# A fused attention-and-MLP layer on Trainium2: a pair's last values are transposed within the next projection, and the high parts of the projections' weights are made in two pieces

## The chip, the cores and the metric

The kernel runs on one core of one Trainium2 chip. The metric is the device time of one execution in microseconds. Before the change three timed runs gave a median of 1065.94 us (1065.62 to 1066.48).

## The reference: what is computed

One layer on a sequence of 1024 tokens of width 1024, all in float32:

```
n  = rms_norm(h, norm1_g)
qa, ka, va, qb, kb, vb = split(n @ w_in)     # 512, 128, 128, 512, 512, 512 columns
ya = mixer_a(qa, ka, va, sinks)              # 8 heads, 2 key heads, window 128, ALiBi, sinks
yb = mixer_b(qb, kb, vb, rel_bias)           # 8 heads, own chunk of 64 and 8 before, learned bias
h  = h + concat(rms_norm(ya), rms_norm(yb)) @ w_out
h  = h + square(relu(rms_norm(h) @ w_ff1)) @ w_ff2
out = rms_norm(h)
```

Both mixers are softmax attention with heads of 64 columns. In group B each query block of 128 rows looks at up to five key blocks.

## The kernel before

**Numbers in two parts.** Every operand of a matmul is kept as a high part (rounded to the format that TensorE reads, `fp32r` in the profile) and a low part (what is left). One product is three matmuls into one accumulator: high by high, high by low, low by high (`mm3`, L129 in the profile). High parts are made by ScalarE (ACT), low parts by VectorE (DVE) or GpSimd (POOL) in `split_l` (L135).

**Stages.** Up to about 46 us the input is loaded and the first projections are made; up to about 394 us attention runs, interleaved with projections; then the second half of the output projection, the first MLP matmul up to about 752 us and the second up to the end.

**Projections.** `in_proj` makes one of queries, keys or values for a pair of heads. It loads a weight of 128x8x128, has ACT make its high part in one instruction of 128x1024 (L172, `w_qB<-st_qB`), POOL its low part in four of 128x256 (L135, through `load_weight`), and then goes over two halves of the tokens and eight k blocks: three matmuls into an accumulator `ip_` per block. Each block is one step of the generator. At the end of a half, `place` scales the result by the tokens' norm on DVE (`ts_`, L246 for values). Values must be turned to have tokens on the partitions: `turn_v` transposes four blocks on TensorE (`vt_`, L132), ACT copies the high part out (L269, `VvB`), DVE subtracts for the low part (L135, `VvB`). The first half's values are turned within the second half at k block 2. The second half's are turned after two empty steps, and so right ahead of the next projection's first matmuls. Fifteen projections go through `in_proj`: the queries of A's pairs 1 to 3, and keys, queries, values (kB, qB, vB) of B's four pairs.

**Attention.** `UnitA` and `UnitB` are pieces of attention. For each block of queries there are scores (`S_`), a bias and a row minimum on DVE (`P_`, L412 or L414), the exponential on ACT (L415), the division by the row sum on DVE or POOL (L589, L521), transposes of the probabilities on TensorE (`pt_`), their eviction in two parts, ACT first and DVE second (`T_`, L422 and L135), and the products with the values (`av_`). A `pt_` of group B, numbered 0 to 7 within a unit, is filled by up to four transposes, and is free again only when ACT and DVE have both read it.

**What sets the order.** TensorE's order is the program's order, held by hand (`pe_order`). A queue `Filler` deals out steps of projections between the steps of attention: `interleave` runs one step of a unit, sometimes a score of the next, and then some filler steps. `finish(name)` runs filler until a pair's projections are done. The last projection in the queue is followed by `out_proj_a`, the first half of the output projection (`op_A_`). The order on ACT, DVE, POOL and on SP's queue of DMAs is chosen by the Tile scheduler. In group B's stage accumulators `ip_` or `op_A_`, `pt_` and `vt_` share three PSUM banks (tag `w`, `bufs=3`), handed out by rotation as the scheduler finds them free.

**Places.** The second half of a B pair's values is turned four times: at about 145 us (pair 0, within group A's last units; called place 1), 202 us (pair 1, place 2), 260 us (pair 2, place 3) and 316 us (pair 3, place 4, where the filler has come to `op_A_`).

Of the kernel before, what the change touches and what calls it, by code (L numbers as in the profile page):

```python
# [45 lines left out]
def kernel(  # L46
# [26 lines left out]
    nc = tc.nc  # L73
# [10 lines left out]
    def page(shape, name, dt=F32R):  # L84
        return main.tile(shape, dt, tag="pg", bufs=NPAGES, name=name)
# [69 lines left out]
    def mm3(ps, a, b, start, stop, shared=False):  # L155

        matmul(ps, a[0], b[0], start=start, stop=False, skip_group_check=shared)
        matmul(ps, a[0], b[1], start=False, stop=False, skip_group_check=shared)
        matmul(ps, a[1], b[0], start=False, stop=stop, skip_group_check=shared)

    def load_weight(src, shape, name, low_engine, cuts=1, pieces=1):

        st = stage(shape, f"st_{name}")
        w = [page(shape, f"w{hl}_{name}") for hl in range(2)]

        def steps():
            n = shape[1] // cuts
            for i in range(0, shape[1], n):
                load(st[:, i : i + n], src[:, i : i + n])
                for j in range(i, i + n, n // pieces):  # L170
                    c = slice(j, j + n // pieces)
                    nc.scalar.activation(w[0][:, c], st[:, c], AF.Copy)  # L172
                    width = shape[2] if len(shape) > 2 else 1
                    short = min(n // pieces, LOW_COLS // width) if low_engine is nc.gpsimd else n // pieces
                    for k in range(j, j + n // pieces, short):
                        c = slice(k, k + short)
                        split_l(low_engine, w[1][:, c], st[:, c], w[0][:, c])
                yield

        if cuts > 1:  # L180
            return w, steps()
        for _ in steps():
            pass
        return w
# [47 lines left out]
    def project(acc, w, t, ks=range(NK)):  # L232
        for k in ks:
            n = [nT[t][hl][k // 2][:, k % 2, :] for hl in range(2)]
            mm3(acc, (w[0][:, k], w[1][:, k]), n, k == 0, k == NK - 1)

    def place(acc, kind, name, dst, t, low_engine, st=None):
        if st is not None:
            pass
        elif name == "vA":  # L240
            st = page([P, 2, HALF], f"ts_{name}_{t}")
        else:
            st = main.tile([P, 2, HALF], F32R, tag="tst", bufs=2, name=f"ts_{name}_{t}")
        c = slice(t * HALF, (t + 1) * HALF)
        if kind == "v":
            nc.vector.tensor_tensor(f(st[:, 0]), acc, R1[:, c], ALU.mult)  # L246
            return lambda *where: turn_v(st, name, dst, t, *where)
        if kind[0] == "q":
            nc.vector.scalar_tensor_tensor(f(st[:, 1]), acc, HD**-0.5, R1[:, c], ALU.mult, ALU.mult)
        else:  # L250
            nc.vector.tensor_tensor(f(st[:, 1]), acc, R1[:, c], ALU.mult)
        nc.scalar.activation(st[:, 0], f(st[:, 1]), AF.Copy)
        split_l(low_engine, st[:, 1], f(st[:, 1]), st[:, 0])
        for hl in range(2):
            for s in range(2):
                src = f(st[s * HD : (s + 1) * HD, hl])
                if kind == "q":
                    last = nc.sync.dma_start(f(dst[s][hl * HD : (hl + 1) * HD, c]), src)
                else:
                    for rep in range(2):  # L260
                        last = nc.sync.dma_start(f(dst[2 * hl + s][rep * HD : (rep + 1) * HD, c]), src)
        return last.ins.name
# [9 lines left out]
    def proj_weight(c0, name, low_engine, *cuts):  # L272
        return load_weight(w_in[:, c0 : c0 + P].rearrange("(k p) c -> p k c", p=P), [P, NK, P], name, low_engine, *cuts)
# [10 lines left out]

    def in_proj(c0, kind, name, dst, new):

        w = proj_weight(c0, name, nc.gpsimd)
        yield
        later = None
        for t in range(2):  # L290
            acc = aps.tile([P, HALF], F32, tag="w", bufs=3, name=f"ip_{name}_{t}")
            for k in range(NK):
                project(acc, w, t, (k,))
                if k == 2 and later:
                    later(aps, "w", 3)
                if k == NK - 1:
                    if t == 0:
                        dst.extend(new(name))
                    later = place(acc, kind, name, dst, t, nc.gpsimd)
                    later = later if kind == "v" else None  # L300
                yield
        if later:
            yield
            yield
            later(aps, "w", 3)

    dve, pool = nc.vector, nc.gpsimd
    KA, VA, Q = new_k("A"), new_v("A"), new_q("A0")
# [42 lines left out]
    project(accs[1], wts[1], 1)  # L351
    Qs = [Q, [], [], []]
    ahead_A1 = in_proj(QA0 + P, "q", "qA1", Qs[1], new_q)
    next(ahead_A1)
    last_load[0] = turns[1]
# [10 lines left out]
    aps = ap_.enter_context(tc.tile_pool(name="aps", bufs=1, space=PSUM, reuse_waits="tile"))  # L366
# [60 lines left out]
    class Pair:  # L427
# [34 lines left out]
        def finish(self, t):  # L462

            Y, yc = self.out[t]
            c = slice(t * HALF, (t + 1) * HALF)
            if self.j == 0 and t == 0:
                sq[self.kind] = page([P, SEQ], f"sq{self.kind}", F32)
            acc = sq[self.kind][:, c]
            if self.j == 0:
                nc.gpsimd.tensor_tensor(acc, Y, Y, ALU.mult)  # L470
            elif self.m == 7 and t == 1:
                nc.scalar.activation(yc, Y, AF.Square)
                nc.vector.tensor_tensor(acc, acc, yc, ALU.add)
            else:
                y2 = page([P, HALF], f"y2{t}_{self.m}", F32)
                nc.gpsimd.tensor_tensor(y2, Y, Y, ALU.mult)
                nc.gpsimd.tensor_tensor(acc, acc, y2, ALU.add)
            if self.y is None:
                y = page([P, 2, HALF], f"y{t}_{self.m}")
                split_y(y, Y, self.m)  # L480
                nc.sync.dma_start(yd[self.m, :, t], f(y))
            else:
                split_y(self.y[t], Y, self.m)
# [176 lines left out]
    def load_y(m):  # L660
        y = new_y(m)
        for t in range(2):
            nc.sync.dma_start(f(y[t]), yd[m, :, t])
        return y

    def out_weight(m):
        return load_weight(w_out[m * P : (m + 1) * P, :], [P, D], f"o{m}", pool, 1, 2)
# [3 lines left out]
    def out_proj_step(ps, ys, ws, q, tb, c):  # L671
        y = ys[q][tb // 4][:, :, tb % 4 * P : (tb % 4 + 1) * P]
        mm3(ps, (y[:, 0], y[:, 1]), [v[:, c] for v in ws[q]], q == 0, q == 3)

    class Filler:
# [28 lines left out]
                self.step()  # L704

        def finish(self, name):
            while any(q[0] == name for q in self.queue):
                self.step()

    def interleave(unit, nexts, n_fill):  # L710
# [11 lines left out]
    def out_proj_a():  # L722
        ys, ws = [], []
        for m in range(4):
            ws.append(out_weight(m))
            if m > 1:
                ys += [load_y(2 * m - 4), load_y(2 * m - 3)]
        yield
        for tb in range(TB):
            h = hres[tb] = page([P, D], f"h{tb}", F32)  # L730
            nc.sync.dma_start(h, x[tb * P : (tb + 1) * P, :])
            for dh in range(2):
                c = slice(dh * HALF, (dh + 1) * HALF)
                ps = aps.tile([P, HALF], F32, tag="w", bufs=3, name=f"op_A_{tb}_{dh}")
                for q in range(4):
                    out_proj_step(ps, ys, ws, q, tb, c)
                    if q == 3:
                        nc.vector.scalar_tensor_tensor(h[:, c], ps, rA[:, tb : tb + 1], h[:, c], ALU.mult, ALU.add)  # L738
                    yield
# [4 lines left out]
    for j in range(4):  # L744
        if j > 1:
            fill.add(f"A{j}", in_proj(QA0 + j * P, "q", f"qA{j}", Qs[j], new_q))
        pair = Pair("A", j, Qs[j], KA, VA)
        units += [(UnitA(pair, i0), f"A{j}", A_FILL) for i0 in range(0, TB, 2)]
    y7 = new_y(7)
    for j in range(4):  # L750
# [4 lines left out]
        pair = Pair("B", j, Q, K, V, y7 if j == 3 else None)  # L755
        units += [(UnitB(pair, s, t), f"B{j}", B_FILL[t] if j < 3 else LAST_FILL[t][s]) for t in range(2) for s in range(2)]
    fill.add("out", out_proj_a())

    ahead = []
# [460 lines left out]
    g, p, n0 = order2[-GQ]  # L1220
# [57 lines left out]
```

## Time and profile before

| | before |
|---|---|
| median of three runs | 1065.94 us |
| the profiled execution, its own time | 1066.38 us |
| its span in the trace | 1064.5 us |
| TensorE (PE) busy | 1047.2 us, 98% |
| DVE busy | 707.2 us, 66% |
| ACT busy | 578.7 us, 54% |
| POOL busy | 415.9 us, 39% |
| mean granted clock of TensorE | 0.999 |

The time of the execution is 1.9 us over the span; what lies around the span is taken as constant. In a timeline's row stand the start in us, the busy time in us, the engine, the line, the operation and its tile as output<-input; `x4` means that four alike in a row are put together; brackets give the idle time of the engine ahead of it and what ended that. The table of waits adds such idle time by what was waited for.

### The profile page before, as it was taken

What the parts mean: (1) busy time and instruction counts of PE and PEld (TensorE: products, weight loads), DVE (VectorE), ACT (ScalarE), POOL (GpSimd) and SP (SyncE); (2) the same over time, 40 slices, a digit from 0 to 9 for tenths busy, and PEclk for the clock granted to TensorE, in tenths of its full rate; (3) what the DMA queues carried; (4) which work ended last, traced back from release to release, by engine and by line L of the source; (5) the groups of instructions that cost most, each with busy time, mean ns of one, the idle gap of its engine ahead of it and who ended that gap; (6) DMA issues with size and microseconds to landing.
All of it is one profiled execution on the core that took longest, in us unless ns stands there. A gap on an engine that the chain in (4) does not pass through costs nothing.

```text
span 1064.5 us, 14392 instructions
## 1 busy us (share of the span) xinstructions
PE 1047.2 (98%) x5040; PEld 873.0 (82%) x5040; DVE 707.2 (66%) x1134; ACT 578.7 (54%) x994; POOL 415.9 (39%) x316
## 2 busy tenths in 40 slices
PE   8999999999999999999999999999999999999997
PEld 6888877888888888888888888888888888888885
DVE  4577887767677765696524335436878777778667
ACT  7676765666574566675544544455533333333346
POOL 1476765244370243405564454345014024024025
PEclk9999999999999999999999999999999999999999
DMA  9955525253575442214544535417997535532004
GB/s 327 265 145 138 160 79 156 92 141 102 136 249 207 139 159 100 96 63 164 192 139 159 177 119 172 164 63 247 376 403 269 164 123 164 181 116 89 1 1 159
DMA packets 90440, 170.17 MB, mean 160 GB/s; under 512 B 7808, under 2 KB 43520, under 8 KB 90368
## 3 DMA queue, kind: packets, MB, share of 16 engines
q1 hardware_dynamic: 90224, 169.25, 48.4%
q8 instruction: 40, 0.66, 0.3%
q14 instruction: 32, 0.26, 0.1%
q10 hardware_dynamic: 144, 0.00, 0.0%
HBM read 105.26 MB, written 45.09 MB: 141 GB/s over the span
## 4 chain that ended last, share of the span: by engine, by line
PE 89%; DVE 5%; DMA 2%; ACT 1%; issue 1%; SPq 0%; POOL 0%; DVEq 0%; ACTq 0%
PE f L129 27%; PE f_a L129 16%; PE f_c L129 8%; PE op_B L129 4%; PE f_b L129 4%; PE op_A L129 4%; PE ip_qB L129 4%; PE ip_qA L129 4%; PE ip_vB L129 3%; PE av_B L129 3%; PE ip_kB L129 3%; PE pt_B L132 2%; PE S_B L129 2%; PE S_A L129 1%; DMA xs<-in_xT_dram 1%
## 5 line engine op out<-in xcount | busy, mean ns | idle before, releaser
L129 PE MATMUL f<-X,W 128*128 128x512 f32 x1344 | 306.0, 389 | 0.0
L129 PEld LDWEIGHTS f<-X,W 128*128 128x128 f32 x1344 | 252.0, 188 | 52.8 <-DVE X L135 0.5
L129 PE MATMUL f_a<-V,U 128*128 128x512 f32 x768 | 176.0, 389 | 0.0
L129 PEld LDWEIGHTS f_a<-V,U 128*128 128x128 f32 x768 | 144.2, 188 | 29.9
L135 POOL TENSOR_TENSOR U<-u,U 128x1024 fp32r<-128x1024 f32 x32 | 79.8, 2494 | 227.4 <-PE f_c L129 135.9
L135 POOL TENSOR_TENSOR W<-T,W 128x1024 fp32r<-128x1024 f32 x29 | 74.7, 2577 | 138.9 <-ACT W L946 138.9
L129 PE MATMUL f_c<-V,U 128*128 128x512 f32 x384 | 88.3, 389 | 0.0
L129 PEld LDWEIGHTS f_c<-V,U 128*128 128x128 f32 x384 | 72.1, 188 | 15.0
L946 ACT ACTIVATE V<-Z 128x1024 fp32r<-128x1024 f32 x32 | 33.9, 1060 | 88.9 <-PE f_a L129 44.6
L135 POOL TENSOR_TENSOR W<-w,W 128x1024 fp32r<-128x1024 f32 x23 | 58.2, 2532 | 32.5 <-ACT W L946 32.0
L135 DVE TENSOR_TENSOR V<-w,V 128x1024 fp32r<-128x1024 f32 x24 | 50.3, 2096 | 30.1 <-ACT V L946 30.1
L946 ACT ACTIVATE V<-w 128x1024 fp32r<-128x1024 f32 x24 | 25.4, 1060 | 80.8 <-issue 34.2
L995 DVE TENSOR_TENSOR k<-f,k 128x1024 f32<-128x1024 f32 x24 | 29.3, 1221 | 59.6 <-PE f L129 59.6
L946 ACT ACTIVATE U<-u 128x1024 fp32r<-128x1024 f32 x56 | 58.5, 1044 | 10.4 <-DMA ud<-k 7.1
L415 ACT ACTIVATE P_B<-P_B,nm_B 128x640 f32<-128x640 f32 (+2 forms) x64 | 44.4, 694 | 25.2 <-DVE nm_B L414 13.1
L989 ACT ACTIVATE k<-f 128x1024 f32<-128x1024 f32 x24 | 24.6, 1026 | 59.2 <-PE f L129 59.2
L135 DVE TENSOR_TENSOR V<-Z,V 128x1024 fp32r<-128x1024 f32 x32 | 48.4, 1516 | 9.3 <-ACT V L946 5.9
L129 PE MATMUL op_A<-w_o,y 128*128 128x512 f32 x192 | 52.1, 397 | 0.5 <-DVE h L738 0.5
L129 PE MATMUL ip_vB<-nT,w_vB 128*128 128x512 f32 x192 | 51.9, 398 | 0.0
L946 ACT ACTIVATE W<-T 128x1024 fp32r<-128x1024 f32 x32 | 33.9, 1059 | 32.9 <-PE f L129 20.7
L129 PE MATMUL ip_qB<-nT,w_qB 128*128 128x512 f32 x192 | 51.5, 396 | 0.0
L129 PE MATMUL ip_kB<-nT,w_kB 128*128 128x512 f32 x192 | 51.3, 396 | 0.0
(212 smaller groups left out, 2031.7 us busy)
## 6 DMA issues: line engine op xcount, KB each, us to landing
w<-in_w_ff_dram SPq DMA_DIRECT2D x64, 512.0 KB, 4.5
u<-ud SPq DMA_DIRECT2D x56, 512.0 KB, 4.4
ud<-k SPq DMA_DIRECT2D x48, 512.0 KB, 3.1
KkB<-ts_kB SPq DMA_DIRECT2D x64, 128.0 KB, 2.3
yd<-y SPq DMA_DIRECT2D x14, 512.0 KB, 2.8
y<-yd SPq DMA_DIRECT2D x14, 512.0 KB, 6.5
xs<-in_xT_dram SPq DMA_DIRECT2D x16, 256.0 KB, 5.5
xr<-in_x_dram SPq DMA_DIRECT2D x8, 512.0 KB, 7.1
```

The costliest lines, as they stand in the source:

```text
L129: pe(nc.tensor.matmul(*args, **kw))
L132: pe(nc.tensor.transpose(*args))
L135: engine.tensor_tensor(lo, full, f(hi), ALU.subtract)
L415: nc.scalar.activation(pr[:, :n], pr[:, :n], AF.Exp, bias=nm, scale=-1.0, accum_out=sm)
L946: nc.scalar.activation(w[0], full, AF.Copy)
L989: nc.scalar.activation(kept[p], ps, AF.Copy)
L995: dve.tensor_tensor(v, ps, v, ALU.add)
```

## The change: when the last values are turned, and the weight's high part in two

First, `in_proj` no longer turns the second half's values itself. It appends the turning to a list `pending`, and `turn_pending` runs it at k block 2 of the next projection, or at the third product of `out_proj_a`. `finish(name)` also steps until the pair's entry is gone from the list. Two empty steps after a values projection stay. Second, `proj_weight` is called with `cuts=1, pieces=2`: ACT makes the high part in two instructions of 128x512, and POOL's first two low parts depend on the first of them alone. There are still four low parts.

```diff
--- before.py
+++ after.py
@@ -284,25 +284,30 @@
 
     def in_proj(c0, kind, name, dst, new):
 
-        w = proj_weight(c0, name, nc.gpsimd)
+        w = proj_weight(c0, name, nc.gpsimd, 1, 2)
         yield
-        later = None
         for t in range(2):
             acc = aps.tile([P, HALF], F32, tag="w", bufs=3, name=f"ip_{name}_{t}")
             for k in range(NK):
                 project(acc, w, t, (k,))
-                if k == 2 and later:
-                    later(aps, "w", 3)
+                if k == 2:
+                    turn_pending()
                 if k == NK - 1:
                     if t == 0:
                         dst.extend(new(name))
                     later = place(acc, kind, name, dst, t, nc.gpsimd)
-                    later = later if kind == "v" else None
+                    if kind == "v":
+                        pending.append((name[1:], later))
                 yield
-        if later:
+        if kind == "v":
             yield
             yield
-            later(aps, "w", 3)
+
+    pending = []
+
+    def turn_pending():
+        while pending:
+            pending.pop()[1](aps, "w", 3)
 
     dve, pool = nc.vector, nc.gpsimd
     KA, VA, Q = new_k("A"), new_v("A"), new_q("A0")
@@ -704,7 +709,7 @@
                 self.step()
 
         def finish(self, name):
-            while any(q[0] == name for q in self.queue):
+            while any(q[0] == name for q in self.queue) or any(p[0] == name for p in pending):
                 self.step()
 
     def interleave(unit, nexts, n_fill):
@@ -734,6 +739,8 @@
                 ps = aps.tile([P, HALF], F32, tag="w", bufs=3, name=f"op_A_{tb}_{dh}")
                 for q in range(4):
                     out_proj_step(ps, ys, ws, q, tb, c)
+                    if q == 2:
+                        turn_pending()
                     if q == 3:
                         nc.vector.scalar_tensor_tensor(h[:, c], ps, rA[:, tb : tb + 1], h[:, c], ALU.mult, ALU.add)
                     yield
```

On TensorE nothing else moves than the four `vt_` at each of the four places. At place 2 its rows before the change (the last number of a name counts tiles; a line of dots leaves rows out: more matmuls of `ip_kB`, and more transposes into the same `pt_`):

```order
L132 MATMUL pt_B_1_2_2527<-ident,P_B_1_2_2432 128x128
L129 MATMUL av_B_1_2534<-padF_557,VvB_1765 128x256 x2
L132 MATMUL vt_vB_1_2537<-ident,ts_vB_1_2506 128x128 x4
L129 MATMUL ip_kB_0_2553<-nT_155,w_kB_2339 128x512
...
L132 MATMUL pt_B_1_3_2560<-ident,P_B_1_0_2393 128x128
...
L129 MATMUL av_B_1_2534<-T_B_1_1_2511,VvB_1765 128x256 x2
L129 MATMUL S_B_1_1_2570<-KkB_1314,QqB_1548 128x320 x2
...
L129 MATMUL ip_kB_0_2553<-nT_156,w_kB_2339 128x512
...
L132 MATMUL pt_B_1_4_2583<-ident,P_B_1_0_2393 128x128
...
L129 MATMUL av_B_1_2534<-T_B_1_2_2531,VvB_1765 128x384 x2
```

And with the change at the same place:

```order
L132 MATMUL pt_B_1_2_2537<-ident,P_B_1_2_2442 128x128
L129 MATMUL av_B_1_2544<-padF_558,VvB_1772 128x256 x2
L129 MATMUL ip_kB_0_2557<-nT_155,w_kB_2348 128x512
...
L132 MATMUL pt_B_1_3_2564<-ident,P_B_1_0_2403 128x128
...
L129 MATMUL av_B_1_2544<-T_B_1_1_2521,VvB_1772 128x256 x2
L129 MATMUL S_B_1_1_2574<-KkB_1319,QqB_1554 128x320 x2
...
L129 MATMUL ip_kB_0_2557<-nT_156,w_kB_2348 128x512
...
L132 MATMUL vt_vB_1_2587<-ident,ts_vB_1_2516 128x128 x4
L132 MATMUL pt_B_1_4_2594<-ident,P_B_1_0_2403 128x128
...
L129 MATMUL av_B_1_2544<-T_B_1_2_2541,VvB_1772 128x384 x2
```

The four transposes move from ahead of `ip_kB_0`'s first matmul to behind its ninth, right ahead of `pt_B_1_4`. The same holds at places 3 and 4 (there behind nine matmuls of `op_A_0`). At place 1 they move behind nine matmuls of `ip_kB_0` too, and stand ahead of the 512-wide `av_A_0`.

On ACT the scheduler changes more. At place 2 before (`w_qB` is the high part of the next projection's weight, `T_` the evictions, `P_` the exponentials):

```order
L647 ACTIVATE y_4_2492<-Y_0_2361,ogc 128x512
L422 ACTIVATE T_B_1_2_2531<-pt_B_1_2_2527 128x384
L269 ACTIVATE VvB_2419<-vt_vB_1_2537 128x8x64
L415 ACTIVATE P_B_1_0_2518,sm_B_1_2515<-P_B_1_0_2518,nm_B_1_2514 128x640
L422 ACTIVATE T_B_1_3_2565<-pt_B_1_3_2560 128x512
L172 ACTIVATE w_qB_2545<-st_qB_2544 128x1024
L422 ACTIVATE T_B_1_4_2588<-pt_B_1_4_2583 128x512
L415 ACTIVATE P_B_1_1_2571,sm_B_1_2515<-P_B_1_1_2571,nm_B_1_2514 128x640
L415 ACTIVATE P_B_1_2_2594,sm_B_1_2515<-P_B_1_2_2594,nm_B_1_2514 128x640
L422 ACTIVATE T_B_1_5_2610<-pt_B_1_5_2606 128x384
```

And with the change, where lines after 310 are numbered 5 or 7 higher:

```order
L652 ACTIVATE y_4_2502<-Y_0_2371,ogc 128x512
L427 ACTIVATE T_B_1_2_2541<-pt_B_1_2_2537 128x384
L172 ACTIVATE w_qB_2548<-st_qB_2547 128x512 x2
L420 ACTIVATE P_B_1_0_2528,sm_B_1_2525<-P_B_1_0_2528,nm_B_1_2524 128x640
L427 ACTIVATE T_B_1_3_2569<-pt_B_1_3_2564 128x512
L420 ACTIVATE P_B_1_1_2575,sm_B_1_2525<-P_B_1_1_2575,nm_B_1_2524 128x640
L427 ACTIVATE T_B_1_4_2599<-pt_B_1_4_2594 128x512
L427 ACTIVATE T_B_1_5_2621<-pt_B_1_5_2617 128x384
L420 ACTIVATE P_B_1_2_2605,sm_B_1_2525<-P_B_1_2_2605,nm_B_1_2524 128x640
L427 ACTIVATE T_B_1_6_2635<-pt_B_1_6_2632 128x256
L427 ACTIVATE padL_559<-pt_B_1_7_2643 128x128
L269 ACTIVATE VvB_2429<-vt_vB_1_2587 128x8x64
```

`w_qB`, now two instructions, moves from behind `T_B_1_3` to ahead of `P_B_1_0`; `VvB` moves from ahead of `P_B_1_0` to behind `padL`. At place 3 `w_qB` takes the same place, where it stood behind `P_B_1_0`, and `VvB` moves ahead of `T_B_1_4`. At place 4 there is no `w_qB`, and `VvB` moves from ahead of `P_B_1_0` to ahead of `P_B_1_1`, both ahead of `T_B_1_4`.

At place 1, ACT's rows before:

```order
L415 ACTIVATE P_A_4_1_1920,sm_A_4_1884<-P_A_4_1_1920,nm_A_4_1883 128x256
L269 ACTIVATE VvB_1766<-vt_vB_1_1896 128x8x64
L415 ACTIVATE P_A_4_1_1920,sm_A_4_1884<-P_A_4_1_1920,nm_A_4_1883 128x256
L516 ACTIVATE es_A_4_1929<-nm_A_4_1883,psink 128x2
L560 ACTIVATE yc_0_1947<-av_A_0_1916 64x256
L172 ACTIVATE w_qB_1904<-st_qB_1903 128x1024
L422 ACTIVATE T_A_2_0_1959<-pt_A_2_0_1958 128x512
L560 ACTIVATE yc_0_1947<-av_A_0_1916 64x256
L422 ACTIVATE T_A_2_1_1970<-pt_A_2_1_1969 128x512
L415 ACTIVATE P_A_6_0_1981,sm_A_6_1978<-P_A_6_0_1981,nm_A_6_1977 128x256 x2
L516 ACTIVATE es_A_6_2027<-nm_A_6_1977,psink 128x2
```

And with the change:

```order
L420 ACTIVATE P_A_4_1_1921,sm_A_4_1891<-P_A_4_1_1921,nm_A_4_1890 128x256
L172 ACTIVATE w_qB_1904<-st_qB_1903 128x512 x2
L420 ACTIVATE P_A_4_1_1921,sm_A_4_1891<-P_A_4_1_1921,nm_A_4_1890 128x256
L521 ACTIVATE es_A_4_1930<-nm_A_4_1890,psink 128x2
L565 ACTIVATE yc_0_1955<-av_A_0_1917 64x256
L427 ACTIVATE T_A_2_0_1967<-pt_A_2_0_1966 128x512
L565 ACTIVATE yc_0_1955<-av_A_0_1917 64x256
L427 ACTIVATE T_A_2_1_1978<-pt_A_2_1_1977 128x512
L269 ACTIVATE VvB_1773<-vt_vB_1_1945 128x8x64
L420 ACTIVATE P_A_6_0_1989,sm_A_6_1986<-P_A_6_0_1989,nm_A_6_1985 128x256 x2
L521 ACTIVATE es_A_6_2035<-nm_A_6_1985,psink 128x2
```

`w_qB` moves four instructions up, in between two exponentials of `P_A_4_1`, and `VvB` moves behind `T_A_2_1`.

DVE's part of `VvB` moves with ACT's. At places 2 and 3 the bias step `P_B_1_1` (L412) also moves ahead of `T_B_1_3` on DVE; at place 4 DVE's `VvB` and `P_B_1_2` now stand between `T_B_1_3` and `T_B_1_4`. At place 1 POOL's four low parts of `w_qB` move ahead of its share of `P_A_4`'s division.

The banks of tag `w` fall otherwise too. At place 2 `pt_B_1_3` and `pt_B_1_4` were in two different banks and are now in one, which `pt_5` to `pt_7` use as well, while `vt_vB_1` holds another until its late eviction. At places 3 and 4 `pt_3` and `pt_4` are in one bank as well, and `pt_5` takes that of `vt_vB_1`; at place 4 `op_A_0_1` takes the bank of `pt_4`.

## Prediction

> **What bounds the kernel now.** I read the page first, then TensorE's waits, then the busy time by stretch, then the timeline around the four places. The page's first part:
>
> ```profile
> PE 1047.2 (98%) x5040; PEld 873.0 (82%) x5040; DVE 707.2 (66%) x1134; ACT 578.7 (54%) x994; POOL 415.9 (39%) x316
> ```
>
> TensorE (PE) is busy for 98% of the span, so a change that leaves its matmuls alone can win only what PE idles, and loses what it adds in waits. PE's waits, with total, times and longest in us:
>
> ```profile
> PE ip_kA L129 <- ACT w_kA L172: 5.0, 1, 5.0
> PE av_A L129 <- DVE Y L561: 1.3, 1, 1.3
> PE vt_vB L132 <- DVE ts_vB L246: 0.8, 1, 0.8
> PE S_B L129 <- DVE T_A L135: 0.6, 1, 0.6
> PE pt_B L132 <- DVE T_B L135: 0.3, 2, 0.2
> ```
>
> The 5.0 us are the program's start and use other code. No other weight is waited for: the earlier low parts that the two pieces allow are worth nothing on PE. One `vt_vB` in four waits, for 0.8 us. The busy time by stretch (length, then busy us of PE, its weight loads, DVE, ACT, POOL) says where:
>
> ```profile
> 140.00:180.00 40.00, 36.81 (x201) 30.63 (x200) 32.42 (x89) 25.98 (x71) 21.46 (x25) 1.00 0.44 129
> 180.00:220.00 40.00, 39.84 (x221) 33.87 (x220) 26.47 (x66) 23.80 (x51) 14.37 (x18) 1.00 0.33 95
> 220.00:260.00 40.00, 40.00 (x230) 34.50 (x229) 26.81 (x73) 25.46 (x54) 13.96 (x17) 1.00 0.45 122
> ```
>
> Place 1 lies in a stretch with 3.2 us idle, all that could be won; places 2 to 4 lie in stretches without slack, where each new wait is added to the end in full.
>
> **The change part by part: the prices.** ACT and DVE by shape (count, busy us and mean ns of one, idle before):
>
> ```profile
> L172 ACT ACTIVATE w_qB<-st_qB 128x1024 fp32r<-128x1024 f32 x4 | 4.2, 1062 | 1.6 <-DMA yd<-y 0.9 <-POOL sqB L477 0.4
> L172 ACT ACTIVATE w_o<-st_o 128x512 fp32r<-128x512 f32 x14 | 8.0, 622 | 1.8 <-DMA st_o<-in_w_out_dram 1.1 <-PE S_B L129 0.7
> L422 ACT ACTIVATE T_B<-pt_B 128x512 fp32r<-128x512 f32 x24 | 14.2, 593 | 8.7 <-PE pt_B L132 8.2
> L415 ACT ACTIVATE P_B<-P_B,nm_B 128x640 f32<-128x640 f32 x32 | 26.4, 827 | 11.6 <-DVE nm_B L412 11.4
> L412 DVE CUSTOM_DVE_ANT_0 P_B<-S_B,b_B 128x640 f32<-128x640 f32 x32 | 26.0, 816 | 4.8 <-PE S_B L129 4.6
> L135 DVE TENSOR_TENSOR T_B<-pt_B,T_B 128x512 fp32r<-128x512 f32 x24 | 16.5, 686 | 12.3 <-ACT T_B L422 12.2
> L135 DVE TENSOR_TENSOR VvB<-vt_vB,VvB 128x512 fp32r<-128x512 f32 x8 | 5.5, 684 | 1.6 <-ACT VvB L269 1.6
> ```
>
> A high part in two pieces costs 2 x 0.622 = 1.244 us against 1.062, so 0.18 more; fifteen times, 2.7 us of ACT, which is busy for 54% and idle beside PE: free, except where the eviction of a `pt_` stands behind it. The four transposes cost PE the same wherever they stand.
>
> **Place 1.** Rows of the timeline before:
>
> ```profile
> 145.64 0.65 PE L132 MATMUL vt_vB<-ident,ts_vB 128*128 128x128 f32 x4 [0.78 <-DVE ts_vB L246]
> 146.06 0.42 DVE L135 TENSOR_TENSOR T_A<-pt_A,T_A 128x256 fp32r<-128x256 f32 x1
> 146.82 0.40 PE L129 MATMUL av_A<-T_A,VA 128*128 128x256 f32 x2
> 151.87 1.06 ACT L172 ACTIVATE w_qB<-st_qB 128x1024 fp32r<-128x1024 f32 x1
> 155.11 0.42 DVE L561 TENSOR_TENSOR Y<-av_A,yc 64x256 f32<-64x256 f32 x1
> 155.68 0.71 PE L129 MATMUL av_A<-T_A,VA 128*128 128x256 f32 x4 [1.34 <-DVE Y L561]
> 162.45 0.50 PE L129 MATMUL S_B<-KkB,QqB 128*128 128x256 f32 x2 [0.57 <-DVE T_A L135]
> ```
>
> Without `vt` there, PE goes on to `ip_kB`, but `av_A` then waits for DVE's `T_A`, done at 146.06 + 0.42 = 146.48. It starts at about 146.5, 0.3 earlier, and the transposes (0.36 from start to next start at place 2, below) come back behind it: nothing gained by 149. The 1.34 us end with `Y` on DVE at 155.5. With `w_qB` 1.8 us earlier on ACT, and `Y` ahead of two bias steps, I work `Y`'s end out at about 155.0, so `av_A` at 155.1, 0.55 earlier. But those bias steps, the exponentials behind them and then `VvB` (0.69) move later by as much, on the chain that ends with DVE's `T_A` before `S_B` at 162.45; I get 162.6. Net +0.1. The bounds: -1.9 if both 1.34 and 0.57 go, +0.8 if `VvB` falls into the chain in full with its 0.69.
>
> **Place 2.** Rows before:
>
> ```profile
> 201.67 0.60 PE L132 MATMUL vt_vB<-ident,ts_vB 128*128 128x128 f32 x4
> 202.03 1.62 PE L129 MATMUL ip_kB<-nT,w_kB 128*128 128x512 f32 x6
> 202.28 0.47 ACT L422 ACTIVATE T_B<-pt_B 128x384 fp32r<-128x384 f32 x1
> 203.81 0.66 PE L132 MATMUL pt_B<-ident,P_B 128*128 128x128 f32 x4 [0.16 <-DVE T_B L135]
> 204.54 0.76 PE L129 MATMUL S_B<-KkB,QqB 128*128 128x320 f32 x4
> 205.13 0.86 PE L129 MATMUL ip_kB<-nT,w_kB 128*128 128x512 f32 x3
> 205.83 0.60 PE L132 MATMUL pt_B<-ident,P_B 128*128 128x128 f32 x4
> 206.02 1.06 ACT L172 ACTIVATE w_qB<-st_qB 128x1024 fp32r<-128x1024 f32 x1 [0.92 <-DMA yd<-y]
> ```
>
> The two `pt_B` are `pt_3` and `pt_4`. Six matmuls take 1.39 from their start to the next start (322.40 to 323.79 at place 4, below). With the change they start at 201.67, and `pt_3`, now in a bank that is free by then, at 203.06. The scores follow at 203.06 + 0.73 = 203.79, the three matmuls at 204.38, `vt` at 205.08, and PE reaches `pt_4` at 205.44. But `pt_4` is now in `pt_3`'s bank, and must wait for `pt_3`'s eviction. ACT ends `T_2` at 202.75, makes `w_qB` in 1.24 up to 203.99, then the exponential (0.83, and 0.19 to read its sum) up to 205.0, then `T_3` (0.59) up to 205.6. DVE adds 0.69: 206.3, and `pt_4` at 206.35. DVE's bias step ahead of `T_3` takes 0.82 from the scores' end, 203.79 + 0.76 = 204.55, and is over at 205.5 with the reading and the reciprocal: just in time. So +0.52 against 205.83. From there `pt_5` to `pt_7` share the bank too, but their evictions are shorter than the 2 us of PE between them, so nothing more. The bounds: 0, if the scheduler's order meets a slower PE; +1.2, if `pt_3` is not earlier (first rival).
>
> The row puts the old wait at `pt_3` at 0.16; by the starts it is 203.81 - 202.03 - 1.39 = 0.39. I use starts throughout. The Trainium skill (Perfetto Trace Analysis, Tensor Engine Instruction) says that a matmul's end in a profile is estimated and not observed; by the printed idle time alone the price of this place would be some 0.2 higher, 0.7. The Trainium skill (PSUM — Partial Sum Buffer, PSUM bank collisions) also has a rule that speaks against the change: no two engines may be at one bank at once, so a matmul into a bank must stand behind all readers. By that alone, one bank for all `pt_` would cost nothing here, as 0.36 + 0.59 + 0.69 = 1.64 us is under the 2.02 us between `pt_3` and `pt_4`; the rows above say that it is what ACT has ahead of the eviction that makes it a wait.
>
> **Place 3.** The same positions, 57.88 us later:
>
> ```profile
> 262.34 1.06 ACT L172 ACTIVATE w_qB<-st_qB 128x1024 fp32r<-128x1024 f32 x1 [0.41 <-POOL sqB L477]
> 263.71 0.60 PE L132 MATMUL pt_B<-ident,P_B 128*128 128x128 f32 x4
> ```
>
> Before, `w_qB` already stood ahead of `T_3`, but `pt_4` was in another bank. After, the same sum as at place 2: `pt_4` at 264.2, +0.5 (bounds 0 and +1.2).
>
> **Place 4.** Before:
>
> ```profile
> 319.27 0.68 DVE L135 TENSOR_TENSOR T_B<-pt_B,T_B 128x512 fp32r<-128x512 f32 x1
> 319.54 0.60 PE L132 MATMUL pt_B<-ident,P_B 128*128 128x128 f32 x4
> 320.32 0.75 PE L129 MATMUL S_B<-KkB,QqB 128*128 128x320 f32 x4
> 322.40 1.55 PE L129 MATMUL op_A<-w_o,y 128*128 128x512 f32 x6
> 323.79 0.38 PE L132 MATMUL pt_B<-ident,P_B 128*128 128x128 f32 x2
> 325.17 0.33 PE L132 MATMUL pt_B<-ident,P_B 128*128 128x128 f32 x1
> ```
>
> There is no `w_qB` here, and `pt_4` comes on time, at 319.5. But DVE now does `VvB` and the next bias step between `T_3` and `T_4`: that bias step starts with the scores' end at 321.05, and with 0.82, its reading, a reciprocal and `T_4` (0.69) DVE is done at 322.7. `op_A`'s next accumulator takes `T_4`'s bank: 322.75 against 322.40. The division and the exponential that `T_5` stands behind put `pt_6` at 324.55, and `pt_7` at 325.9: +0.75 against 325.17 (bounds 0 and +1.0).
>
> **The sum.** 0.1 + 0.5 + 0.5 + 0.75 = +1.85 us. After place 4 PE is busy nearly throughout, and its few waits there hang on chains that move along, so nothing takes this back. Against the profiled execution, 1066.38, that is 1068.2; it lies 0.44 over the median of the runs, so against the median, 1065.94, it is 1067.8. A measurement of this kernel can tell about 0.2%, 2.1 us, from no change: 1067.8 is a loss too small to tell.
>
> **The rivals.**
>
> *Slower by more than 0.2%: the eviction of `pt_3` stands behind the bias step as well.* If `pt_3` at places 2 and 3 still starts near 203.81, because its bank or its probabilities come no sooner, the next scores end at 205.3 and not 204.55. DVE does their bias step ahead of `T_3` (0.82, reading and reciprocal 0.28, then 0.69): 207.05, and `pt_4` is 1.2 late. Twice 1.2, with +0.75 and +0.1, is +3.25: 1069.2. It decides from a `pt_3` at 203.2 or later, 0.15 us past my sum. For it: DVE and ACT run in a fixed order, so each lateness is passed on. Against it: the bank of `pt_3` was released by a `T_1` that in the trace before was done by 201.9. Chance 0.36, with all that adds up to over +2.1.
>
> *Faster by more than 0.2%: place 1 gives its idle time back.* The waits of 0.78, 1.34 and 0.57 go, 2.7 us, if the early `w_qB` also speeds what ends at 162.45, and places 2 to 4 cost under 0.3 together since ACT's order has slack I don't see: -2.4, 1063.5. For it: three waits in one stretch. Against it: the price there is a chain over ACT and DVE, to which the change only adds. Chance 0.14.
>
> *Nothing happens.* The transposes are covered wherever they stand, the pieces are hidden behind an idle ACT, and what place 1 wins places 2 to 4 lose: 1065.9. Chance 0.15, within the same verdict as my forecast, whose own chance is 0.35.
>
> **How the numbers follow.** Forecast 1067.8. Within 0.2% is 0.35 + 0.15 = 0.50, slower 0.36, faster 0.14. The sum of the upper bounds, 0.8 + 1.2 + 1.2 + 1.0 = 4.2, gives 1070.1; the lower, -1.9, gives 1064.0. All at one end at once is unlikely, so these hold 8 in 10 with the faster rival mostly left out: 1064.0 to 1070.1.
>
> **What would show it.** Right: the 0.8 us wait of `vt_vB` is gone; `pt_B <- DVE T_B` has grown to about 0.9 us at places 2 and 3 each, with `pt_4` 0.5 late by the starts; op_A waits for `T_B` near 322. Wrong: no such wait, or `pt_3` still near 203.8 (counted from `av_B`), or `w_qB` finishing before `T_2`; a stretch 140 to 180 that is over 1 us shorter in idle time would speak for the faster rival.

## The result, and the profile after

The changed kernel takes 1068.41 us (nine runs, 1068.06 to 1069.02) against 1065.94 us before (nine runs, 1065.43 to 1067.25): a ratio of 1.0024, 95% interval 1.0016 to 1.0033. That is +2.47 us, where +1.85 was forecast, and 0.24%: a small loss, but one that the interval tells from no change. The profiled execution of the changed kernel took 1068.81 us, with a span of 1067.0 us.

The page's first part, and TensorE's waits (total, times, longest in us):

```profile
PE 1048.8 (98%) x5040; PEld 873.6 (82%) x5040; DVE 707.3 (66%) x1134; ACT 580.6 (54%) x1009; POOL 416.4 (39%) x316
```

```profile
PE av_A L129 <- DVE Y L566: 1.6, 2, 1.0
PE pt_B L132 <- DVE T_B L135: 1.1, 2, 0.6
PE S_B L129 <- DVE T_A L135: 0.9, 1, 0.9
PE op_A L129 <- DVE T_B L135: 0.2, 1, 0.2
PE pt_B L132 <- DVE VvB L135: 0.2, 1, 0.2
```

The 0.8 of `vt_vB` is gone. `pt_B` behind DVE's `T_B` has grown from 0.3 to 1.1, and two waits are new, of `op_A` for `T_B` and of `pt_B` for `VvB`. The busy time by stretch says that the loss is in the attention:

```profile
140.00:180.00 40.00, 36.86 (x199) 30.34 (x198) 31.80 (x86) 25.89 (x71) 21.01 (x25) 1.00 0.46 129
180.00:220.00 40.00, 39.45 (x219) 33.40 (x218) 26.15 (x67) 24.09 (x53) 14.45 (x18) 1.00 0.36 103
```

The first stretch, with place 1, is as full as before (36.81 then). The second, with place 2, was at 39.84.

To put a price on each place I take stretches of TensorE's order between fixed points: the first transpose of each pair's first turning (138.27, 195.82, 253.68 and 309.81 us before; 138.11, 195.95, 254.31 and 311.19 after), then `pt_7` at place 4 (325.17; 327.58), then the end of the span. TensorE's work between two such points is the same in both kernels, since the four transposes move within one stretch only. All lengths are in us:

| kernel | up to place 1 | place 1 | place 2 | place 3 | place 4 | rest | span |
|---|---|---|---|---|---|---|---|
| before | 138.27 | 57.55 | 57.86 | 56.13 | 15.36 | 739.33 | 1064.5 |
| after | 138.11 | 57.84 | 58.36 | 56.88 | 16.39 | 739.42 | 1067.0 |
| difference | -0.16 | +0.29 | +0.50 | +0.75 | +1.03 | +0.09 | +2.5 |
| forecast | 0 | +0.1 | +0.5 | +0.5 | +0.75 | 0 | +1.85 |

The four places make +2.57 together, which is the whole result. Nothing takes it back behind place 4, as forecast (the span is printed to 0.1 us, so the +0.09 of the rest is nothing).

### The profile page after: what moved, and what is told of

It reads as the page before. It is cut to its first block, busy times and chain, and to the rows that moved or that the text cites. A ratio compares the mean times of both kernels' runs of the same rounds, so it can differ in the third digit from the quotient of the medians.

```text
span 1067.0 us, 14413 instructions
## 1 busy us (share of the span) xinstructions
PE 1048.8 (98%) x5040; PEld 873.6 (82%) x5040; DVE 707.3 (66%) x1134; ACT 580.6 (54%) x1009; POOL 416.4 (39%) x316
## 4 chain that ended last, share of the span: by engine, by line
PE 86%; DVE 5%; issue 3%; DMA 2%; ACT 2%; POOL 1%; SPq 1%; DVEq 0%; ACTq 0%; POOLq 0%
PE f L129 27%; PE f_a L129 16%; PE f_c L129 8%; PE op_B L129 4%; PE f_b L129 4%; PE ip_qB L129 4%; PE op_A L129 4%; PE ip_vB L129 3%; PE ip_kB L129 3%; PE av_B L129 3%; PE S_B L129 2%; PE pt_B L132 2%; PE ip_qA L129 2%; PE av_A L129 1%; PE S_A L129 1%
## 5 line engine op out<-in xcount | busy, mean ns | idle before, releaser
L135 DVE TENSOR_TENSOR V<-w,V 128x1024 fp32r<-128x1024 f32 x24 | 47.3, 1974 | 27.2 <-ACT V L953 27.2
L427 ACT ACTIVATE T_B<-pt_B 128x512 fp32r<-128x512 f32 (+2 forms) x72 | 34.9, 485 | 31.3 <-PE pt_B L132 30.9
```

The lines of the kernel that those rows point to most:

```text
L135: engine.tensor_tensor(lo, full, f(hi), ALU.subtract)
L427: nc.scalar.activation(T[:, 0, lo:hi], tp, AF.Copy)
```

## The experiments

The theory after the result: each place costs what the table says, through an eviction that `pt_4` and what follows it wait for, and the high parts in two pieces cost nothing. Rivals: the pieces cost it; the shared bank alone costs it, whatever stands ahead of the eviction; the four places are one delay that is carried along; and, for what was not forecast, DVE waits beside POOL. Two short names: `T_3` is the eviction of `pt_3`, first on ACT and then on DVE, and `P_1_0` and `P_1_1` are the first and second block of the unit whose scores are being made meanwhile.

The stretches of all kernels stand here once. The columns are those of the table above without the first and the rest, which lies between 739.30 and 739.42 in all of them:

| kernel | place 1 | place 2 | place 3 | place 4 | time, us | ratio to before |
|---|---|---|---|---|---|---|
| before, second profile | 57.40 | 57.84 | 56.10 | 15.67 | 1066.86, one run | |
| after, second profile | 57.85 | 58.35 | 56.86 | 16.52 | 1068.55, one run | |
| pieces alone | 56.56 | 57.84 | 56.08 | 15.37 | 1065.01 | 0.9995 (0.9986 to 1.0004) |
| deferral alone | 56.65 | 58.34 | 56.85 | 16.40 | 1067.29 | 1.0015 (1.0006 to 1.0024) |
| `w_qB` late at places 2, 3 | 57.85 | 57.47 | 56.13 | 16.40 | 1067.01 | 1.0014 (1.0005 to 1.0023) |
| pair 3 as before | 57.85 | 58.36 | 56.84 | 15.36 | 1067.58 | 1.0019 (1.0010 to 1.0027) |
| `T_3` ahead of the bias step | 57.83 | 58.25 | 56.61 | 16.42 | 1068.46, one run | |
| POOL light, places 1 and 4 | 57.21 | 58.30 | 56.85 | 15.92 | 1067.78 | 1.0020 (1.0011 to 1.0029) |
| POOL light, place 3 | 57.86 | 58.34 | 56.44 | 16.40 | 1068.39, one run | |
| pieces, deferral for pair 1 alone | 56.72 | 57.46 | 56.10 | 15.38 | 1065.31 | 0.9993 (0.9985 to 1.0002) |

The kernel before, run beside them, took 1065.62 us beside the four from "pieces alone" to "pair 3 as before", 1065.90 beside "POOL light, places 1 and 4" and the last one, and 1066.65 (one run) beside the two others with one run.

**Two more profiles.** The kernels before and after, unchanged.

> The kernel before once more, for a second profile. If the stretches between fixed points are properties of the kernel, they come out again within 0.1 us: 57.55 us from pair 0's first turning to pair 1's, then 57.86, 56.13 and 15.36.

> The changed kernel once more, for a second profile: the stretches again within 0.1 us, 57.84, 58.36, 56.88 and 16.39.

Places 1 to 3 repeat within 0.15 us, and place 4 within 0.31 before and 0.13 after, which is more than the 0.1 expected. By the second pair of profiles the four places cost 0.45, 0.51, 0.76 and 0.85 us. The 0.31 lies ahead of place 4's own matmuls: `op_A`'s first starts 316.68 - 310.08 = 6.60 behind pair 3's first turning, against 316.11 - 309.81 = 6.30 in the first profile. What differs from run to run is the time up to place 1: 137.52 to 138.74 over all traces, in no order with the kernels. So a stretch tells a few tenths of a us, and the span alone does not.

**Pieces alone.** The kernel before, with one edit:

```diff
-        w = proj_weight(c0, name, nc.gpsimd)
+        w = proj_weight(c0, name, nc.gpsimd, 1, 2)
```

> The kernel before with the two pieces alone; the values are turned where they were. Theory (the banks and what stands ahead of an eviction are the cost): the order on TensorE, ACT and DVE is almost that of before, the 0.18 us more of ACT per weight lies beside other work, so 0.0 us, within 0.4. Rival (the pieces cost, by 15 times 0.18 us on ACT and POOL's other order): most of the 2.5 us of the full change.

Places 2 to 4 are as before, so the pieces cost nothing there. Place 1 is 0.99 shorter, which the prediction had no term for. Part of it comes from DVE's order, which the scheduler changed at place 1 though the edit changes only how the weights are prepared: two bias steps now stand ahead of an eviction `T_A` for which DVE had sat idle. A row of the kernel before, and one with the pieces alone:

```profile
153.58 0.69 DVE L135 TENSOR_TENSOR T_A<-pt_A,T_A 128x512 fp32r<-128x512 f32 x1 [0.50 <-ACT T_A L422]
```

```profile
154.64 0.71 PE L129 MATMUL av_A<-T_A,VA 128*128 128x256 f32 x4 [0.75 <-DVE Y L561]
```

The wait of `av_A` for `Y` is 0.75 and not 1.34, and it starts 154.64 - 137.78 = 16.86 behind pair 0's first turning, against 155.68 - 138.27 = 17.41. So 0.55 of the 0.99 is there already.

**Deferral alone.** The changed kernel, with the high parts in one piece:

```diff
-        w = proj_weight(c0, name, nc.gpsimd, 1, 2)
+        w = proj_weight(c0, name, nc.gpsimd)
```

> The later turning alone; each high part in one instruction of 128x1024. Theory: w_qB still stands ahead of the eviction of pt_3 at places 2 and 3, with 1.06 us in place of 1.24, so 0.18 less at each of the two, 0.36 us less than the full change: +2.1 us against the kernel before. Rival (the pieces cost): 0 us.

Places 2, 3 and 4 cost the same as in the full change, within 0.03: the deferral makes their loss. The longer `w_qB`, for which 0.18 less was expected at each of places 2 and 3, does not show. Place 1 is 0.90 shorter than before. So each half of the change wins about 0.9 at place 1, and both together lose 0.3: the halves do not add up there.

**`w_qB` late.** The changed kernel, in which the next projection is made ready only after six steps of `kB2` and `kB3`, so that ACT makes `w_qB` behind `T_3` at places 2 and 3. TensorE's order and the bank that `pt_3` and `pt_4` share stay. DVE's order changes with ACT's: the division of `P_1_0` and then `T_3` come ahead of the bias step again. At place 2 `pt_5` and `pt_7` also fall into another bank than `pt_4`:

```diff
+                late = self.queue[0][0] in ("B2", "B3") and self.queue[0][3] and self.taken < 6
-                self.ready(2)
+                self.ready(1 if late else 2)
+                self.taken += 1
```

> The full change, but at places 2 and 3 the queries' weight is readied six steps later, so that ACT makes w_qB behind the eviction of pt_3; TensorE's order and the shared bank of pt_3 and pt_4 stay. Theory (it is w_qB ahead of that eviction that makes the shared bank a wait): the waits of 0.80 us before pt_4 at each of the two places go, and the 0.33 us for VvB at place 3 goes, since VvB moves ahead too: 0.55 us over the kernel before, between 0.2 and 1.0. Rival (the shared bank alone, or the four transposes right ahead of pt_4, make the wait): still +2.5 us.

Place 3 is back at 56.13, and place 2 at 57.47 is 0.39 shorter than before the change. The four stretches make +0.95 us, within the 0.2 to 1.0 expected; the median is +1.39, outside it. The rows at place 2 of this kernel:

```profile
202.97 0.60 PE L132 MATMUL pt_B<-ident,P_B 128*128 128x128 f32 x4
203.61 0.60 ACT L427 ACTIVATE T_B<-pt_B 128x512 fp32r<-128x512 f32 x1
204.24 0.69 DVE L135 TENSOR_TENSOR T_B<-pt_B,T_B 128x512 fp32r<-128x512 f32 x1
204.85 0.81 DVE L417 CUSTOM_DVE_ANT_0 P_B<-S_B,b_B 128x640 f32<-128x640 f32 x1
204.93 0.60 PE L132 MATMUL vt_vB<-ident,ts_vB 128*128 128x128 f32 x4
205.37 0.60 PE L132 MATMUL pt_B<-ident,P_B 128*128 128x128 f32 x4
```

`T_3` is over at 204.93 and `pt_4` starts at 205.37, 0.44 behind `vt`, where it was 206.29 - 205.14 = 1.15 in the changed kernel. The shared bank alone is no wait; what stands ahead of the eviction is, on ACT and DVE together, since both orders changed here. From pair 1's first turning `pt_4` starts after 9.63, against 10.34 with the change and 10.01 before. The 0.38 to before agrees with the 0.39 by the starts that `pt_3` waited there: the idea of the change works at place 2 when ACT's order lets it.

**Pair 3 as before.** The changed kernel, in which `vB3` is turned behind its two empty steps:

```diff
             yield
             yield
+        if name == "vB3":
+            turn_pending()
```

> The full change, but pair 3's values (place 4) are turned where they were before; all else is the same order. Theory: place 4 has its own waits, about 1.0 us (from 1.39 us late at its start to 2.41 us late at its end): +1.5 us against the kernel before. Rival (lateness of the earlier places carries on into place 4, which costs nothing itself): still +2.5 us.

Place 4 is back at 15.36 with places 1 to 3 unchanged. Its 1.03 is its own, and not a delay from earlier places.

**`T_3` ahead of the bias step.** The changed kernel, with an order on DVE alone: at places 2 and 3 the bias step `P_1_1` has to stand behind `T_3`. The scheduler then puts the division `P_1_0` ahead of `T_3` at both.

```diff
+            if behind:
+                dep = mybir.DependencyInfo(mybir.DependencyClass.NoSync, mybir.DependencyReason.DATA)
+                tc.add_manual_dep(low.ins, last_T[0], dep, reason="program order")
```

> The full change with DVE's bias step put behind its part of T_3 at places 2 and 3; the scheduler then puts the division of P_1_0 ahead of T_3. Theory (w_qB on ACT makes the sums of P_1_0 late, so that what DVE has to do ahead of T_3 ends late either way): DVE's T_3 starts 0.07 us sooner at most, and place 2 stays at 58.3 us (0.45 over before). Rival (the bias step's place on DVE alone makes the wait): pt_4 comes 0.27 us sooner, when ACT's part of T_3 ends, and place 2 is 58.1 us.

Place 2 is at 58.25, so 0.11 of its 0.50 is gone: another DVE instruction takes the place of the bias step, and ACT's `T_3` is hardly earlier. Place 3 gains 0.27, since `VvB` now stands at 265.40 instead of 266.37. So neither the theory (58.3 at place 2) nor the rival (58.1) holds in full: the bias step's place is a part of the wait. On ACT one instruction behind `pt_4` also changed its place at each of the two. One run, so these are bounds rather than prices.

**POOL light at places 1 and 4.** The changed kernel, in which POOL fills the low parts of `w_qB1` with zeros instead of subtracting them (place 1), and leaves out one addition of squares to `sqB` (place 4). The low part of that weight, and the squares of one pair's outputs over half of the tokens, are missing from what is computed. The orders of TensorE, ACT and DVE stay.

```diff
-                        split_l(low_engine, w[1][:, c], st[:, c], w[0][:, c])
+                        if name == "qB1":
+                            nc.gpsimd.memset(f(w[1][:, c]), 0.0)
+                        else:
+                            split_l(low_engine, w[1][:, c], st[:, c], w[0][:, c])
...
-                nc.gpsimd.tensor_tensor(acc, acc, y2, ALU.add)
+                if (self.m, t) != (6, 0):
+                    nc.gpsimd.tensor_tensor(acc, acc, y2, ALU.add)
```

> The full change with POOL's work made light at two places, and the same order on TensorE, ACT and DVE: at place 1 the low part of pair 1's query weight is set to zero by four fills instead of four subtractions, and at place 4 POOL's addition of one half's squares to the group's sum is left out. Theory (DVE's divisions by the row sum run long while POOL computes beside them: 1.66 us for two of 128x256 at place 1, 1.39 us for one of 128x640 at place 4): place 1 gets about 1.0 us shorter, place 4 about 0.5 us, so +1.0 us against the kernel before. Rival (DVE's long divisions have nothing to do with POOL, or lie off the chain that ends last): still +2.5 us.

Place 1 is 0.63 shorter than after the change (1.0 expected) and place 4 is 0.47 shorter (0.5 expected). At place 4 of the changed kernel:

```profile
318.72 1.65 POOL L482 TENSOR_TENSOR sqB<-sqB,y 128x512 f32<-128x512 f32 x1
319.33 1.39 DVE L594 TENSOR_SCALAR P_B<-P_B,rc_B 128x640 f32<-128x640 f32 x1
320.64 0.68 DVE L135 TENSOR_TENSOR T_B<-pt_B,T_B 128x512 fp32r<-128x512 f32 x1
321.37 0.66 PE L132 MATMUL pt_B<-ident,P_B 128*128 128x128 f32 x4
324.65 1.62 PE L129 MATMUL op_A<-w_o,y 128*128 128x512 f32 x6 [0.19 <-DVE T_B L135]
327.58 0.32 PE L132 MATMUL pt_B<-ident,P_B 128*128 128x128 f32 x1
```

And with POOL light:

```profile
318.02 0.55 DVE L598 TENSOR_SCALAR P_B<-P_B,rc_B 128x640 f32<-128x640 f32 x1
318.52 0.69 DVE L135 TENSOR_TENSOR T_B<-pt_B,T_B 128x512 fp32r<-128x512 f32 x1
319.65 0.60 PE L132 MATMUL pt_B<-ident,P_B 128*128 128x128 f32 x4
```

The same division takes 1.39 us beside POOL's addition and 0.55 without it. From the first turning of pair 3 (309.88 in this kernel, 311.19 above) `T_3` starts after 8.64 instead of 9.45, and `pt_4` after 9.77 instead of 10.18 (9.73 before the change). So `pt_4` is on time here, and the 0.56 that place 4 still costs comes behind it: `op_A` waits for `T_4`, 0.19 as printed, as in the changed kernel. At place 1 the wait of `av_A` for `Y` (1.01) is gone, but `S_B` waits 1.3 instead of 0.9, so that only part of it reaches the end.

**POOL light at place 3.** The same fill for the low parts of `w_qB3`, whose low part is missing from what is computed:

```diff
+                        if name == "qB3":
+                            nc.gpsimd.memset(f(w[1][:, c]), 0.0)
```

> The full change with the low part of pair 3's query weight set to zero by four fills on POOL in place of four subtractions (place 3); the order on the other engines is the same. Theory (two divisions on DVE that run 1.05 and 0.84 us beside POOL's subtractions, 0.54 us without, hold up VvB, for which pt_5 waits 0.33 us): that wait goes, and the stretch of place 3 is 56.5 us and not 56.88; pt_4 stays as late. Rival (VvB is late by its place in DVE's order alone): 56.88 again.

Place 3 is at 56.44, 0.44 shorter (one run). The rows at place 3 of the changed kernel, and then with POOL light:

```profile
263.03 3.07 POOL L135 TENSOR_TENSOR w_qB<-st_qB,w_qB 128x256 fp32r<-128x256 f32 x4
263.87 0.67 DVE L135 TENSOR_TENSOR T_B<-pt_B,T_B 128x512 fp32r<-128x512 f32 x1
264.45 1.05 DVE L594 TENSOR_SCALAR P_B<-P_B,rc_B 128x640 f32<-128x640 f32 x1
264.68 0.63 PE L132 MATMUL pt_B<-ident,P_B 128*128 128x128 f32 x4 [0.55 <-DVE T_B L135]
265.61 0.84 DVE L594 TENSOR_SCALAR P_B<-P_B,rc_B 128x640 f32<-128x640 f32 x1
266.37 0.68 DVE L135 TENSOR_TENSOR VvB<-vt_vB,VvB 128x512 fp32r<-128x512 f32 x1
267.11 0.55 PE L132 MATMUL pt_B<-ident,P_B 128*128 128x128 f32 x3 [0.16 <-DVE VvB L135]
```

```profile
264.28 0.55 DVE L597 TENSOR_SCALAR P_B<-P_B,rc_B 128x640 f32<-128x640 f32 x1
264.51 0.63 PE L132 MATMUL pt_B<-ident,P_B 128*128 128x128 f32 x4 [0.55 <-DVE T_B L135]
264.94 0.55 DVE L597 TENSOR_SCALAR P_B<-P_B,rc_B 128x640 f32<-128x640 f32 x1
265.55 0.69 DVE L135 TENSOR_TENSOR VvB<-vt_vB,VvB 128x512 fp32r<-128x512 f32 x1
266.62 0.49 PE L132 MATMUL pt_B<-ident,P_B 128*128 128x128 f32 x3
```

`pt_4` waits as before, 0.55 as printed: that is the eviction of `pt_3`. `pt_5` waits no more: its wait was for `VvB`, which stood behind two divisions that POOL had made long.

**Pieces everywhere, deferral for pair 1 alone.** What the runs so far spoke for: the pieces, and the deferral only where it won, with `w_qB` late there.

```diff
+        if name in ("vB0", "vB2", "vB3"):
+            turn_pending()
...
-                self.ready(2)
+                late = self.queue[0][0] == "B2" and self.queue[0][3] and self.taken < 6
+                self.ready(1 if late else 2)
+                self.taken += 1
```

> Two pieces everywhere; the later turning for pair 1 alone (place 2), with the queries' weight that follows readied six steps later. Theory (by the earlier runs' stretches: place 1 with pieces alone -0.99 us, place 2 with the late weight -0.39 us, places 3 and 4 as before): -1.4 us against the kernel before. Rival (those stretches are scatter of single profiles): 0.0 us.

By the stretches it wins 0.83 at place 1 and 0.40 at place 2. By the clock it takes 1065.31 us against 1065.90 in the same comparison: its interval holds 1, so it is not shown to beat the kernel before.

## Why the prediction was right, and where it was not

Its direction holds, and so does its cause at places 2 to 4: an eviction that ends late, with nothing won back. At place 1 the cause was another, and the near agreement there is luck. The forecast called the loss too small to tell, and that did not hold: the interval lies above 1, and the 0.24% lies past the 0.2% from which the slower rival (0.36) counted, with the interval, 0.16% to 0.33%, on both sides of it. That rival named DVE's bias step ahead of `T_3`, which was indeed the last link at place 2, but it needed a late `pt_3`, which did not come. Place by place:

**Place 1** (forecast +0.1, measured +0.29). `vt_vB`'s wait of 0.78 went, as worked out, and 0.63 of it came back at 146.01 as a wait of `av_A` for `Y`. But the sum there took DVE's and ACT's durations for fixed. DVE's division at 152.5 was 1.66 us long in the changed kernel and 0.59 with the deferral alone, with nearly the same work of POOL beside it:

```profile
151.77 2.99 POOL L135 TENSOR_TENSOR w_qB<-st_qB,w_qB 128x256 fp32r<-128x256 f32 x4 [3.34 <-ACT es_A L521]
152.51 1.66 DVE L526 TENSOR_SCALAR P_A<-P_A,rc_A 128x256 f32<-128x256 f32 x2
155.37 0.71 PE L129 MATMUL av_A<-T_A,VA 128*128 128x256 f32 x4 [1.01 <-DVE Y L566]
```

```profile
151.40 3.24 POOL L135 TENSOR_TENSOR w_qB<-st_qB,w_qB 128x256 fp32r<-128x256 f32 x4 [3.35 <-ACT es_A L521]
152.05 0.59 DVE L526 TENSOR_SCALAR P_A<-P_A,rc_A 128x256 f32<-128x256 f32 x2
```

The forecast had `av_A` 0.58 sooner than before (155.1 against 155.68) and `S_B` 0.15 later. Counted from pair 0's first turning, 138.27 before and 138.11 after, `av_A` came 0.15 sooner (17.26 against 17.41) and `S_B` 0.23 later (24.41 against 24.18). So the step that failed is the gain at `av_A`: the division ate it. With the deferral alone `av_A` comes at 153.84 - 137.72 = 16.12, 1.14 sooner than with both. DVE's order around the division is the same in these two kernels: the instruction is the same, and where it falls beside POOL's decides. That the two halves win 0.9 each and lose 0.3 together is of this kind in part, and in part DVE's other order with the pieces alone. The faster rival, that place 1 gives its idle time back, would have had 0.90 of its 2.7 us with the deferral alone.

**Place 2** (forecast +0.5, measured +0.50). The rows of the changed kernel:

```profile
201.80 1.55 PE L129 MATMUL ip_kB<-nT,w_kB 128*128 128x512 f32 x6
202.77 1.14 ACT L172 ACTIVATE w_qB<-st_qB 128x512 fp32r<-128x512 f32 x2
203.19 0.60 PE L132 MATMUL pt_B<-ident,P_B 128*128 128x128 f32 x4
203.81 0.82 ACT L420 ACTIVATE P_B<-P_B,nm_B 128x640 f32<-128x640 f32 x1
204.62 0.58 ACT L427 ACTIVATE T_B<-pt_B 128x512 fp32r<-128x512 f32 x1
204.65 0.82 DVE L417 CUSTOM_DVE_ANT_0 P_B<-S_B,b_B 128x640 f32<-128x640 f32 x1 [0.78 <-PE S_B L129]
205.14 0.60 PE L132 MATMUL vt_vB<-ident,ts_vB 128*128 128x128 f32 x4
205.47 0.67 DVE L135 TENSOR_TENSOR T_B<-pt_B,T_B 128x512 fp32r<-128x512 f32 x1
206.29 0.63 PE L132 MATMUL pt_B<-ident,P_B 128*128 128x128 f32 x4 [0.55 <-DVE T_B L135]
```

`pt_3` starts 1.39 behind `ip_kB`, as worked out, so the slower rival's point (0.15 us past the sum) was not reached. ACT's order was right too, but its rows follow closer than I added them up: from start to next start the two pieces of `w_qB` take 203.81 - 202.77 = 1.04 (1.24 in the sum) and the exponential 204.62 - 203.81 = 0.81 (1.02 in the sum, with the reading of its own), so `T_3` is over on ACT at 205.20 and not at 205.6. DVE was not free then: the bias step held it up to 205.47. So the last link was the scores' end and DVE's bias step, the chain that the sum had as "just in time", and not `w_qB`'s length; that fits with one piece instead of two changing nothing. `pt_4` is late by 206.29 - 205.83 = 0.46, of which 0.13 was there at pair 1's first turning (195.95 against 195.82), so 0.33 and not 0.52; another 0.17 is added in small steps up to the next fixed point. That the total agrees so well is luck, with a part of it mislaid. With `w_qB` behind `T_3` both links go, and so does the loss.

The wait was printed as 0.55; by the starts it is 206.29 - 205.14 - 0.35 = 0.80, with the transposes' 0.35 as in the kernel before, or 0.71 against the 0.44 of the kernel with `w_qB` late (forecast: about 0.9). The rule that a matmul's end in a profile is estimated (the Trainium skill, Perfetto Trace Analysis, Tensor Engine Instruction) agrees with that. The Trainium skill (PSUM — Partial Sum Buffer, PSUM bank collisions raise a hardware error) says that no two engines may access one bank in the same cycle. So a matmul into a shared bank has to stand behind the bank's readers. The kernel with `w_qB` late agrees: DVE has read `pt_3` by 204.93, and `pt_4` comes into the same bank at 205.37 without a wait in its row.

**Place 3** (forecast +0.5, measured +0.75). `pt_4` waits as at place 2, and counted from pair 2's first turning it is (264.68 - 254.31) - (263.71 - 253.68) = 0.34 late, where the sum had 0.5. The step that failed is "nothing more" behind `pt_4`: the sum had `pt_5` in `pt_3`'s bank in mind, where it was in that of `vt_vB`, as the change's own description said, and so behind `VvB`, which DVE must have read. `pt_5` starts 267.11 - 264.68 = 2.43 behind `pt_4`, and 266.62 - 264.51 = 2.11 with POOL light, so 0.32 of the place's loss is that wait.

**Place 4** (forecast +0.75, measured +1.03). The step that failed is "`pt_4` comes on time, at 319.5". It shares `pt_3`'s bank here as well, and DVE's `T_3` was over only at 319.27 + 0.68 = 319.95 before. It could have been earlier, since `VvB` no longer stands ahead of the division. It was not, and these rows of the kernel before say why:

```profile
317.51 1.49 POOL L477 TENSOR_TENSOR sqB<-sqB,y 128x512 f32<-128x512 f32 x1
317.76 0.68 DVE L135 TENSOR_TENSOR VvB<-vt_vB,VvB 128x512 fp32r<-128x512 f32 x1
318.55 0.80 DVE L589 TENSOR_SCALAR P_B<-P_B,rc_B 128x640 f32<-128x640 f32 x1
```

The division ends 0.35 behind POOL's addition in both kernels: 319.35 - 319.00 before, 320.72 - 320.37 after. POOL's addition itself ends 9.19 and 9.18 behind pair 3's first turning. What `VvB` gave free was spent waiting for POOL. So `pt_4` is 321.37 - 319.54 = 1.83 late, 1.38 of it from earlier places, and 0.45 its own; the kernel with POOL light takes back 0.47. What is left there, 0.56, is the part that the sum did have, put at 0.75: `op_A` loses 0.35 to DVE's late `T_4`, as worked out, but `pt_6` only 0.11 more, where the sum had 0.41. So a part that was too high and one that was missing nearly met.

In sum, the terms were off by 0.19, 0, 0.25 and 0.28, all low, and each hides parts that were off by more. The medians of the six experiments with eleven runs, each against the kernel before beside them, lie 0.3 to 0.7 us over what their stretches add up to against its trace (+1.96 against +1.51 with pair 3 as before, +1.88 against +1.38 with POOL light at places 1 and 4); the two with one run lie 0.4 under. What that is stays open, and no place is priced from it.

## What to carry to other kernels

Moving work on TensorE to cover a wait is priced on the engines that empty its accumulators: read what the scheduler then puts ahead of each eviction, and which accumulators fall into one bank. A wait that looks like a bank's can be cured by the order of one weight's preparation on ACT, with what the scheduler then moves on DVE (0.89 us at place 2). Where DVE stands beside POOL, work taken off DVE may be worth nothing, as at place 4, so look at POOL's rows before a DVE duration enters a sum.

## What the runs showed of the hardware

In these traces some DVE instructions that start while POOL is in one end with POOL's, whatever their own length. The 128x4 addition of `sm_A`, 0.16 us when alone, beside POOL's `ts_kB` in three kernels (before, pieces alone, POOL light at places 1 and 4):

```profile
158.66 1.28 POOL L135 TENSOR_TENSOR ts_kB<-ts_kB 128x512 fp32r<-128x512 f32 x1
158.74 1.22 DVE L517 TENSOR_TENSOR sm_A<-sm_A,es_A 128x4 f32<-128x4 f32 x1 [0.94 <-ACT es_A L516]
```

```profile
156.82 1.29 POOL L135 TENSOR_TENSOR ts_kB<-ts_kB 128x512 fp32r<-128x512 f32 x1
157.72 0.42 DVE L517 TENSOR_TENSOR sm_A<-sm_A,es_A 128x4 f32<-128x4 f32 x1 [0.94 <-ACT es_A L516]
```

```profile
157.88 1.28 POOL L135 TENSOR_TENSOR ts_kB<-ts_kB 128x512 fp32r<-128x512 f32 x1
158.60 0.57 DVE L526 TENSOR_TENSOR sm_A<-sm_A,es_A 128x4 f32<-128x4 f32 x1 [0.26 <-ACT es_A L525]
```

POOL ends at 159.94, 158.11 and 159.16, and DVE at 159.96, 158.14 and 159.17. So where an instruction falls beside POOL's can cost it up to 1.06 us (1.22 against 0.16). This is a part of why place 1 differs by so much between kernels that differ by little; how much of each such delay reaches TensorE there was not measured one by one. The evictions in these rows are not held up: `T_B`, which reads `pt_B` from PSUM, takes 0.67 within POOL's `w_qB` at place 3, where the division behind it takes 1.05.

The Trainium skill (SBUF — State Buffer, Who interferes with whom) has a rule for it: the port pair that DVE and GpSimd share is locked for a whole instruction, and the order of issue decides who is blocked. The trace agrees, with DVE's ends 0.01 to 0.03 us behind POOL's in the three cases above; the prediction had not drawn on it.
